# Second feed-forward projection of an encoder layer: its operands loaded three steps ahead, its rows by halves, and a longer fill before the first projection

## The chip, the core and the metric

One Trainium2 chip, one of its cores. The metric is the device time in microseconds (us) of one execution; lower is better. TensorE (PE) does matmuls, VectorE (DVE), ScalarE (ACT) and GpSimd (POOL) the elementwise work, SyncE (SP) issues every DMA.

## The reference, cut to what matters

One layer of a streaming encoder for 1024 prompt rows and 128 sample rows of 1024 columns, float32. The change lies in the last of its blocks:

```
x = LN(alpha*x + mixers(x) @ w_out)              # recurrence and sliding-window attention
x = LN(alpha*x + mem_attention(x))
g, u = split(x @ w_ffn_in)                       # 1024 -> 2 x 2816
y = LN(alpha*x + (silu(g) * u) @ w_ffn_out)      # 2816 -> 1024
```

## The kernel before, in words

Nine tiles of 128 rows: eight of the prompt (`TILES`), one of the samples (`SAMPLE`). Every float32 operand is split into a rounded part `hi` and a rest `lo` (`split`: ACT copies, DVE or POOL subtracts), and a product is three matmuls (`mm3`, L96). The feed-forward block works on the prompt by Strassen-Winograd products of halves: seven products stand for eight. So its operands are the blocks A11, A12, A21, A22 of the weights with sums S1 to S4, and B11, B21, B22 of the rows with differences T1 to T4.

The first projection runs over 11 pairs of column tiles (`PAIRS`), one `hidden(ops, i, then)` each: four loads of 512 KB (`a11`, `a21`, `a22`, `a12`), sums on POOL, then seven products of 24 matmuls of 512 columns. The sample rows go through plain matmuls of 128 columns without a split: for the pairs below `FILL` in `filler`, before `hidden(0)`, with weights loaded a second time through the three buffers `w_raw`; for the others in `sample_pair` inside `hidden`, with the weights that lie there. `all_operands` makes the row operands beforehand, four sets of transposes, copies and subtractions, interleaved with `filler` by planned times. The buffers `big` (10 of 4 KB a partition) hold the rows, the stages of the operands and the weights `a`. The activations are stored to `h_scratch` (B11 to T4) and `hs_scratch` (samples).

The second projection runs over parts of two or three pairs (`PARTS`). A part is a block for the rows (0, 1), the products of the samples, and a block for the rows (2, 3); in the last part the rows 2 and 3 have a block each. A block (`blocks`) goes through `steps`, seven products in the banks x, z and w; `operand` loads the product's operand from `h_scratch` into `hq` (2 buffers), ACT rounds it into `hh`, DVE or POOL subtracts into `hl`. After each product `add` adds the bank to the rows `y` on DVE (L1164); the next product that goes into the same bank waits for that. `prepare` loads the weights of a pair (`raw`, 2 x 512 KB), makes four sums on POOL (L1111 to L1114) and eight pairs of hi (ACT L1121) and lo (DVE or POOL L1122). The first two operands and the first two pairs are prepared inside `hidden(10)` by `ahead`.

Instructions stand on each engine, SP included, in a fixed order, which the program's builder chooses by times that it plans; they need not stand in the order of the source. An engine works through its order without overtaking.

## Time and profile before

| what | value |
|---|---|
| median of 3 runs | 1707.23 us (1706.56 to 1713.33) |
| the profiled execution's own time | 1704.64 us |
| its span, first to last instruction | 1702.9 us |
| PE, DVE, ACT, POOL busy | 1620.7, 1134.6, 674.4, 495.7 us |
| mean granted TensorE clock | 0.981 |

The trace is of one execution; outside its span lie 1.7 us. A clock of 1.00 is the level of 2.4 GHz, 0.50 that of 1.2 GHz.

### The profile page before, as it was taken

What the parts mean: (1) busy time and instruction counts of PE and PEld (TensorE: products, weight loads), DVE (VectorE), ACT (ScalarE), POOL (GpSimd) and SP (SyncE); (2) the same over time, 40 slices, a digit from 0 to 9 for tenths busy, and PEclk for the clock granted to TensorE, in tenths of its full rate; (3) what the DMA queues carried; (4) which work ended last, traced back from release to release, by engine and by line L of the source; (5) the groups of instructions that cost most, each with busy time, mean ns of one, the idle gap of its engine ahead of it and who ended that gap; (6) DMA issues with size and microseconds to landing.
All of it is one profiled execution on the core that took longest, in us unless ns stands there. A gap on an engine that the chain in (4) does not pass through costs nothing.

```text
span 1702.9 us, 24403 instructions
## 1 busy us (share of the span) xinstructions
PE 1620.7 (95%) x9065; PEld 1391.3 (82%) x9065; DVE 1134.6 (67%) x2021; ACT 674.4 (40%) x1365; POOL 495.7 (29%) x381
## 2 busy tenths in 40 slices
PE   8999999999999999999979999999999969988896
PEld 7998999999888987889877888888888857766674
DVE  6786788778488666786687454544444665767576
ACT  4543555446443544325263333323222333434321
POOL 1111111111000000000074443332333454676555
PEclk9999999999999999999998999999999988999998
DMA  7443343334974687556362333122222245333342
GB/s 239 143 160 122 102 148 104 98 118 137 314 274 154 197 278 268 198 171 236 115 205 78 104 115 117 66 74 86 95 92 96 93 164 180 105 118 118 103 146 95
DMA packets 114358, 247.91 MB, mean 146 GB/s; under 512 B 11840, under 2 KB 58048, under 8 KB 114240
## 3 DMA queue, kind: packets, MB, share of 16 engines
q1 hardware_dynamic: 114240, 246.36, 43.8%
q8 instruction: 71, 1.16, 0.3%
q14 instruction: 47, 0.39, 0.1%
HBM read 203.65 MB, written 42.60 MB: 145 GB/s over the span
## 4 chain that ended last, share of the span: by engine, by line
PE 77%; DVE 7%; DMA 6%; POOL 5%; ACT 2%; issue 2%; SPq 1%; POOLq 0%; ACTq 0%; DVEq 0%
PE a L96 48%; PE b L96 20%; PE x L96 3%; PE b L100 2%; DMA hq<-h_scratch 2%; PE z L96 1%; DVE w L1122 1%; PE s L96 1%; DMA raw<-in_w_f_dram 1%; PE w L96 1%; DVE y L1164 1%; DMA w_raw<-in_w_out_dram 1%; DMA w_raw<-in_w_fm_dram 1%; DMA w_raw<-in_w_f_dram 1%; DVE w_lo L137 1%
## 5 line engine op out<-in xcount | busy, mean ns | idle before, releaser
L137 DVE TENSOR_TENSOR w_lo<-w_raw,w_hi 128x1024 fp32r<-128x1024 f32 (+1 forms) x169 | 204.8, 1214 | 115.0 <-ACT w_hi L136 114.6
L136 ACT CAST w_hi<-w_raw 128x1024 fp32r<-128x1024 f32 (+1 forms) x169 | 174.6, 1034 | 206.1 <-PE a L96 77.4
L96 PE MATMUL a<-w_hi,q_hi 128*128 128x256 f32 (+1 forms) x576 | 197.4, 344 | 0.8 <-ACT kv_sb L270 0.7
L96 PE MATMUL a<-w_lo,q_hi 128*128 128x256 f32 (+1 forms) x576 | 196.9, 342 | 0.0
L96 PE MATMUL a<-w_hi,q_lo 128*128 128x256 f32 (+1 forms) x576 | 194.7, 338 | 0.0
L96 PE MATMUL a<-q_hi,w_hi 128*128 128x384 f32 x528 | 186.8, 354 | 7.3 <-ACT q_hi L136 4.3
L96 PE MATMUL a<-q_hi,w_lo 128*128 128x384 f32 x528 | 179.9, 341 | 0.0
L96 PE MATMUL a<-q_lo,w_hi 128*128 128x384 f32 x528 | 179.5, 340 | 0.0
L96 PE MATMUL x<-w,hh 128*128 128x512 f32 x344 | 115.0, 417 | 39.5 <-DVE y L1164 23.6
L137 DVE TENSOR_TENSOR w_lo<-a,w_hi 128x1024 fp32r<-128x1024 f32 x43 | 75.0, 1743 | 76.9 <-ACT w_hi L136 76.9
L96 PEld LDWEIGHTS a<-w_hi,q_hi 128*128 128x128 f32 x576 | 108.4, 188 | 15.6 <-ACT kv_sb L270 1.1
L96 PEld LDWEIGHTS a<-w_lo,q_hi 128*128 128x128 f32 x576 | 108.6, 189 | 13.3 <-issue 1.2
L96 PEld LDWEIGHTS a<-w_hi,q_lo 128*128 128x128 f32 x576 | 108.5, 188 | 12.7 <-issue 0.2
L96 PEld LDWEIGHTS x<-w,hh 128*128 128x128 f32 x344 | 66.6, 198 | 62.8 <-ACT hh L1152 15.7
L96 PEld LDWEIGHTS a<-q_hi,w_hi 128*128 128x128 f32 x528 | 100.5, 190 | 12.2 <-ACT q_hi L136 4.6
L699 POOL TENSOR_TENSOR rs<-rs,mhalf 128x1 f32<-128x1 f32 x18 | 17.2, 958 | 301.0 <-DVE rs L698 301.0
L96 PE MATMUL a<-T_h,w_hi 128*128 128x512 f32 x264 | 104.7, 396 | 0.0
L96 PE MATMUL a<-T_l,w_hi 128*128 128x512 f32 x264 | 104.7, 396 | 0.0
L96 PE MATMUL a<-T_h,w_lo 128*128 128x512 f32 x264 | 104.6, 396 | 0.0
L96 PEld LDWEIGHTS a<-q_lo,w_hi 128*128 128x128 f32 x528 | 100.7, 191 | 1.6 <-issue 0.9
L96 PEld LDWEIGHTS a<-q_hi,w_lo 128*128 128x128 f32 x528 | 100.2, 190 | 1.0 <-DVE w_lo L137 0.7
L1152 ACT CAST hh<-hq 128x512 fp32r<-128x512 f32 (+2 forms) x75 | 46.3, 619 | 133.2 <-DMA hq<-h_scratch 117.3
(308 smaller groups left out, 3930.4 us busy)
## 6 DMA issues: line engine op xcount, KB each, us to landing
a<-in_w_f_dram SPq DMA_DIRECT2D x44, 512.0 KB, 5.2
w_raw<-in_w_fm_dram SPq DMA_DIRECT2D x41, 512.0 KB, 3.9
h_scratch<-w_raw SPq DMA_DIRECT2D x55, 256.0 KB, 2.2
hq<-h_scratch SPq DMA_DIRECT2D x54, 256.0 KB, 2.7
w_raw<-in_w_tm_dram SPq DMA_DIRECT2D x24, 512.0 KB, 3.5
w_raw<-in_w_out_dram SPq DMA_DIRECT2D x24, 512.0 KB, 5.7
w_raw<-in_w_mq_dram SPq DMA_DIRECT2D x24, 512.0 KB, 4.2
w_raw<-in_w_mo_dram SPq DMA_DIRECT2D x24, 512.0 KB, 4.4
```

Of the source, the lines that this page charges most:

```text
L96: return self.eng.matmul(out, lhsT, rhs, **kw)
L100: return self.eng.transpose(out, in_, identity)
L136: S.copy(hi, src)
L137: V.tensor_tensor(lo, src, hi.bitcast(F32), op=ALU.subtract)
L699: G.tensor_tensor(rs, rs, mhalf[:, 0:1], op=ALU.pow)
L1122: (G if name in ("A21", "A22") else V).tensor_tensor(lo, src, hi.bitcast(F32), op=ALU.subtract)
L1152: S.copy(hi, q)
L1164: V.scalar_tensor_tensor(y[b, e][:, hs], y[b, e][:, hs], 1.0 if key in y else ALPHA, ps, op0=ALU.mult, op1=ALU.add)
```

## The change

`FILL` goes from 4 to 6: the samples of pairs 4 and 5 move from `hidden(4)` and `hidden(5)` into `filler`. `begin(0)`, the four weight loads of `hidden(0)` and the split of its first, is called before the last set of row operands. In `hidden(10)` the samples come after the last activation, and their store comes later, after the loads of the second projection's rows. These are loaded by halves in the order of use, with the first operand load after four of eight. `operand` becomes `load(n)`, `part_of(n)` and `operand()`: it loads up to three steps ahead of use and splits one step ahead, in a fixed list of turns, with five buffers `hq` of 2 KB a partition. In the last part, the rows 0 and 1 have a block each, as 2 and 3 had.

```diff
--- before.py
+++ after.py
@@ -31,7 +31,7 @@
 TILES = (0, 1, 3, 4, 5, 6, 7, 8)
 SAMPLE = 2
 PAIRS = FT // 2
-FILL = 4
+FILL = 6
 PARTS = ((0, 2), (2, 4), (4, 6), (6, 8), (8, 11))
 
 
@@ -950,16 +950,19 @@
             load(j)
         yield 3500.0
         for j in range(4):
+            if j == 3:
+                begun.append(begin(0))
             operands(ops, j, (got[j], got[j + 4]))
             yield 6000.0
         order.set(ready, 1000.0)
 
-    def sample_gated(i, h, g):
+    def sample_gated(i, h, g, store=True):
 
         S.activation(h, g[0], AF.Tanh, scale=0.5)
         V.scalar_tensor_tensor(h, h, 1.0, g[0], op0=ALU.add, op1=ALU.mult)
         V.scalar_tensor_tensor(h, h, 0.5, g[1], op0=ALU.mult, op1=ALU.mult)
-        nc.sync.dma_start(out=hs_dram[:, i], in_=h)
+        if store:
+            nc.sync.dma_start(out=hs_dram[:, i], in_=h)
 
     def filler(filled):
 
@@ -979,7 +982,7 @@
             yield
         order.set(filled)
 
-    def sample_pair(i, ws):
+    def sample_pair(i, ws, store=True):
 
         ps = bank("b")
         for e in range(2):
@@ -989,25 +992,34 @@
                              start=kt == 0, stop=kt == KT - 1)
         g = ps.rearrange("p (e z t) -> p z e t", e=2, z=2)
         h = hs.rearrange("p (e t) -> p e t", e=2)
-        sample_gated(i, h, [g[:, 0], g[:, 1]])
+        sample_gated(i, h, [g[:, 0], g[:, 1]], store)
 
     def parts_of(src, hi, lo):
         split(src, hi, lo)
         return hi, lo
 
+    begun = []
+
+    def begin(i):
+
+        def wt(name, j):
+            t = big(name)
+            nc.sync.dma_start(out=t, in_=I["w_f1"][i, j])
+            return t
+
+        a11, a21, a22, a12 = wt("a11", 0), wt("a21", 2), wt("a22", 3), wt("a12", 1)
+        return a11, a21, a22, a12, parts_of(a11, *both_parts())
+
+    def both_parts():
+        return tuple(wp.tile([P, 1024], F32R, name=x, bufs=N_W) for x in ("w_hi", "w_lo"))
+
     def hidden(ops, i, then):
 
-        def wt(name, j=None):
-            t = big(name)
-            if j is not None:
-                nc.sync.dma_start(out=t, in_=I["w_f1"][i, j])
-            return t
-
+        a11, a21, a22, a12, first = begun.pop() if begun else begin(i)
         th = [raw_tile() for _ in range(2)]
         m1 = raw_tile()
         m1 = [m1[:, :512], m1[:, 512:]]
-        a11, a21, a22, a12 = wt("a11", 0), wt("a21", 2), wt("a22", 3), wt("a12", 1)
-        s1, s2, s4 = wt("s1"), wt("s2"), wt("s4")
+        s1, s2, s4 = big("s1"), big("s2"), big("s4")
         G.tensor_tensor(s1, a21, a22, op=ALU.add)
         G.tensor_tensor(s2, s1, a11, op=ALU.subtract)
         G.tensor_tensor(s4, a12, s2, op=ALU.subtract)
@@ -1017,7 +1029,7 @@
         X, Z, W = [], [], []
 
         def product(bk, which, w, op, start):
-            pair = parts_of(w, *(wp.tile([P, 1024], F32R, name=x, bufs=N_W) for x in ("w_hi", "w_lo")))
+            pair = first if w is a11 else parts_of(w, *both_parts())
             for z in range(2):
                 if start:
                     bk.append(bank(which))
@@ -1043,7 +1055,7 @@
         last = i == PAIRS - 1
         if FILL <= i and not last:
             sample_pair(i, ((a11, a12), (a21, a22)))
-        s3 = wt("s3") if last else a21
+        s3 = big("s3") if last else a21
         G.tensor_tensor(s3, a11, a21, op=ALU.subtract)
         for z in product(Z, "b", s1, "T1", True):
             S.copy(m1[z], Z[z])
@@ -1071,12 +1083,12 @@
             store(o, src)
         for z in product(X, "a", a22, "T4", False):
             yield
-        if last:
-            sample_pair(i, ((a11, a12), (a21, a22)))
         gated(th[1][:, a], X[0], X[1])
         G.tensor_tensor(t4, th[1][:, a], t2, op=ALU.subtract)
         store("B21", th[1][:, a])
         store("T4", t4)
+        if last:
+            sample_pair(i, ((a11, a12), (a21, a22)), False)
 
     def final_norm(y, gb, st, b, e):
         mv, rs, nb = small("mv", 2), small("rs", 1), small("nb", 1)
@@ -1143,15 +1155,47 @@
         sums = [bank("s") for _ in range(2)]
         gb = []
 
-        def operand(i0, i1, bs, o):
-
-            k, n, c = i1 - i0, len(bs), bs[0] % 2
-            lo, q, hi = (f2.tile([P, 3, 2, P], t, name=x, bufs=m)[:, :k, :n]
-                         for x, t, m in (("hl", F32R, 5), ("hq", F32, 2), ("hh", F32R, 5)))
-            nc.sync.dma_start(out=q, in_=h_dram[bs[0] // 2, OPS.index(o), :, i0:i1, c:c + n])
-            S.copy(hi, q)
-            (G if o in ("T1", "T3", "T4") else V).tensor_tensor(lo, q, hi.bitcast(F32), op=ALU.subtract)
-            return [[(hi[:, i, b], lo[:, i, b]) for i in range(k)] for b in range(n)]
+        steps = (("x", "A11", "B11", True, (0, 0, None)),
+                 ("z", "S1", "T1", True, (1, 1, None)),
+                 ("x", "S2", "T2", False, (1, 0, None)),
+                 ("z", "S4", "B22", False, (1, 0, 1)),
+                 ("x", "S3", "T3", False, (1, 1, 1)),
+                 ("w", "A12", "B21", True, (0, 0, 0)),
+                 ("x", "A22", "T4", False, (0, 1, 0)))
+
+
+        turns = [(part, bs) for part in PARTS[:-1] for bs in ((0, 1), (2, 3))] + [(PARTS[-1], (b,)) for b in range(4)]
+        wanted = [(*part, bs, step[2]) for part, bs in turns for step in steps][2:]
+        loaded, parted = {}, {}
+
+        def load(n):
+            if n < len(wanted) and n not in loaded:
+                i0, i1, bs, o = wanted[n]
+                k, m, c = i1 - i0, len(bs), bs[0] % 2
+                q = f2.tile([P, 512], F32, name="hq", bufs=5)[:, :k * m * P].rearrange("p (i b x) -> p i b x", b=m, x=P)
+                nc.sync.dma_start(out=q, in_=h_dram[bs[0] // 2, OPS.index(o), :, i0:i1, c:c + m])
+                loaded[n] = q
+
+        def part_of(n):
+            if n < len(wanted) and n not in parted:
+                i0, i1, bs, o = wanted[n]
+                k, m, q = i1 - i0, len(bs), loaded[n]
+                hi, lo = (f2.tile([P, 512], F32R, name=x, bufs=5)[:, :k * m * P].rearrange("p (i b x) -> p i b x", b=m, x=P)
+                          for x in ("hh", "hl"))
+                S.copy(hi, q)
+                (G if o in ("T1", "T3", "T4") else V).tensor_tensor(lo, q, hi.bitcast(F32), op=ALU.subtract)
+                parted[n] = [[(hi[:, i, b], lo[:, i, b]) for i in range(k)] for b in range(m)]
+
+        used = [0]
+
+        def operand():
+            n = used[0]
+            used[0] += 1
+            for x in range(n, n + 4):
+                load(x)
+            for x in range(n, n + 2):
+                part_of(x)
+            return parted.pop(n)
 
         def add(b, e, half, ps, bn, which):
             hs = slice(half * 512, half * 512 + 512)
@@ -1167,21 +1211,13 @@
             if bn is not None:
                 V.bn_stats(bn[:, half], y[b, e][:, hs])
 
-        steps = (("x", "A11", "B11", True, (0, 0, None)),
-                 ("z", "S1", "T1", True, (1, 1, None)),
-                 ("x", "S2", "T2", False, (1, 0, None)),
-                 ("z", "S4", "B22", False, (1, 0, 1)),
-                 ("x", "S3", "T3", False, (1, 1, 1)),
-                 ("w", "A12", "B21", True, (0, 0, 0)),
-                 ("x", "A22", "T4", False, (0, 1, 0)))
-
         def blocks(part, bs, gb):
 
             ws = [prepared[i] for i in range(*part)]
             bk = {}
             bn = {(b, e): sm.tile([P, 2, 6], F32, name="bn", bufs=6) for b in bs for e in range(2)} if gb else {}
             for which, w, h, start, (e, half, fin) in steps:
-                for b, hs in zip(bs, ahead.pop((bs[0] + part[0], h), None) or operand(*part, bs, h)):
+                for b, hs in zip(bs, ahead.pop((bs[0] + part[0], h), None) or operand()):
                     if start:
                         bk[which, b] = bank(which)
                     ps = bk[which, b]
@@ -1222,16 +1258,22 @@
         for n, part in enumerate(PARTS):
             last = n == len(PARTS) - 1
             if n == 0:
-                for e in range(2):
+
+                for k, (e, half) in enumerate(((0, 0), (1, 1), (1, 0), (0, 1))):
+                    c2 = slice(half * 512, half * 512 + 512)
                     for b in range(2):
-                        nc.sync.dma_start(out=y[b, e], in_=x2_dram[TILES[b + 4 * e]])
+                        nc.sync.dma_start(out=y[b, e][:, c2], in_=x2_dram[TILES[b + 4 * e]][:, c2])
+                    if k == 1:
+                        load(0)
+                nc.sync.dma_start(out=hs_dram[:, PAIRS - 1], in_=hs.rearrange("p (e t) -> p e t", e=2))
             if last:
                 both = unit(c, "ln_gb").rearrange("p (n x) -> p n x", n=2)
                 gb = [both[:, n] for n in range(2)]
                 for n in range(2):
                     nc.sync.dma_start(out=gb[n], in_=I["ln"][4 + n:5 + n, :].broadcast_to([P, D]))
-            yield from blocks(part, (0, 1), gb)
-            hs = sample_operands(part)
+            for bs in ((0,), (1,)) if last else ((0, 1),):
+                yield from blocks(part, bs, gb)
+            hx = sample_operands(part)
             if n == 0:
                 for e in range(2):
                     for b in range(2, 4):
@@ -1239,7 +1281,7 @@
 
             while len(prepared) < min(part[1] + 1, PAIRS):
                 more()
-            yield from sample(part, hs, n == 0, last)
+            yield from sample(part, hx, n == 0, last)
             if last:
                 ys = unit(c, "ys")[:, :1024]
                 nc.sync.dma_start(out=ys, in_=x2_dram[SAMPLE])
```

## Rows read from the trace of the kernel before

**Rows 1.** The page: busy time of each engine in us, its share of the span, instructions.

```profile
PE 1620.7 (95%) x9065; PEld 1391.3 (82%) x9065; DVE 1134.6 (67%) x2021; ACT 674.4 (40%) x1365; POOL 495.7 (29%) x381
```

**Rows 2.** Busy time by stage: the stretch from the fill to the first steady product, the first projection, the change to the second, the second up to its last part's samples. Columns: stretch, its length, then busy us (instructions) of PE, PEld, DVE, ACT, POOL, granted clock, share and GB/s of the DMA engines.

```profile
884.60:902.80 18.20, 6.92 (x15) 5.01 (x16) 18.10 (x11) 6.79 (x10) 17.21 (x8) 0.62 0.60 184
902.80:1382.40 479.60, 479.60 (x2283) 395.49 (x2282) 248.94 (x256) 152.97 (x208) 183.10 (x96) 1.00 0.26 91
1382.40:1408.20 25.80, 10.56 (x37) 8.17 (x36) 11.41 (x16) 7.40 (x14) 11.13 (x9) 0.67 0.62 213
1408.20:1650.00 241.80, 217.80 (x883) 169.48 (x881) 163.40 (x220) 85.69 (x153) 146.64 (x99) 0.96 0.40 127
```

**Rows 3.** The chain that ended last, one of its pieces: start, us, what, number of matmuls.

```profile
1482.45 2.82 PE x L96 x12
```

**Rows 4.** Order of time around the start of the first projection: start, us, engine, line, operation, tiles, number, and in brackets the engine's idle time before it and what ended it.

```profile
883.58 1.35 SPq L1003 DMA_DIRECT2D a<-in_w_f_dram  x3
...
889.45 1.03 ACT L136 CAST w_hi<-a 128x1024 fp32r<-128x1024 f32 x1
...
890.53 0.80 PE L96 MATMUL a<-B_h,w_hi 128*128 128x512 f32 x1 [5.98 <-ACT w_hi L136]
...
894.96 2.52 DVE L137 TENSOR_TENSOR w_lo<-a,w_hi 128x1024 fp32r<-128x1024 f32 x1
...
897.53 0.80 PE L96 MATMUL a<-B_h,w_lo 128*128 128x512 f32 x1 [5.35 <-DVE w_lo L137]
```

**Rows 5.** The sample matmuls: two weight tiles of the fill, one pair inside `hidden`, PE's waits for the fill's loads (total, times, longest), and the fill's loads on the page (number, KB each, median us from issue to landing).

```profile
877.13 3.89 PE L96 MATMUL a<-both,w_raw 128*128 128x128 f32 x32 [0.58 <-DMA w_raw<-in_w_f_dram]
1375.12 7.31 PE L96 MATMUL b<-both,a 128*128 128x128 f32 x64
PE a L96 <- DMA w_raw<-in_w_f_dram: 1.7, 4, 0.6
w_raw<-in_w_f_dram SPq DMA_DIRECT2D x16, 512.0 KB, 4.2
```

**Rows 6.** Order of time at the change to the second projection: SP's issues, two of the row additions on DVE, the first new operand on ACT, PE.

```profile
1392.44 0.33 SPq L1227 DMA_DIRECT2D y<-x_scratch  x1
1393.82 0.33 SPq L962 DMA_DIRECT2D hs_scratch<-both  x1
1394.24 1.34 SPq L1227 DMA_DIRECT2D y<-x_scratch  x3
1395.63 1.28 SPq L1151 DMA_DIRECT2D hq<-h_scratch  x2
...
1399.28 0.69 DVE L1164 SCALAR_TENSOR_TENSOR y<-y,x 128x512 f32<-128x512 f32 x1 [2.71 <-DMA y<-x_scratch]
1400.58 0.69 DVE L1164 SCALAR_TENSOR_TENSOR y<-y,z 128x512 f32<-128x512 f32 x1 [0.61 <-DMA y<-x_scratch]
...
1402.47 1.30 ACT L1152 CAST hh<-hq 128x512 fp32r<-128x512 f32 x2 [9.60 <-DMA hq<-h_scratch]
...
1403.14 1.22 PE L96 MATMUL x<-w,hh 128*128 128x512 f32 x2 [15.24 <-ACT hh L1152]
```

**Rows 7.** SP's own waits at that place and in the second projection: total, times, longest.

```profile
SPq L1151 <- POOL hl L1153: 101.3, 30, 7.5
...
SPq L1036 <- POOL w_raw L1077: 6.3, 1, 6.3
...
SPq L1227 <- DMA h_scratch<-w_raw: 1.8, 1, 1.8
```

**Rows 8.** PE's waits in the second projection that follow a late operand, in order of time.

```profile
1432.21 0.70 PE L96 MATMUL x<-w,hh 128*128 128x512 f32 x2 [1.35 <-DVE y L1164]
1439.36 1.22 PE L96 MATMUL z<-w,hh 128*128 128x512 f32 x2 [2.70 <-DVE y L1164]
1453.00 0.71 PE L96 MATMUL x<-w,hh 128*128 128x512 f32 x2 [0.78 <-DVE y L1164]
1504.36 0.71 PE L96 MATMUL x<-w,hh 128*128 128x512 f32 x2 [2.23 <-DVE y L1164]
1557.24 0.71 PE L96 MATMUL x<-w,hh 128*128 128x512 f32 x2 [2.52 <-DVE y L1164]
1685.82 0.71 PE L96 MATMUL x<-w,hh 128*128 128x512 f32 x2 [1.84 <-DVE y L1164]
```

**Rows 9.** DVE just before the fifth of these waits ended, in order of time; then the half-clock stretches after the second and the fifth, as in Rows 2.

```profile
1554.13 0.69 DVE L1153 TENSOR_TENSOR hl<-hq,hh 128x512 fp32r<-128x512 f32 x1 [4.31 <-ACT hh L1152]
...
1556.42 0.67 DVE L1164 SCALAR_TENSOR_TENSOR y<-y,x 128x512 f32<-128x512 f32 x1
...
1438.70:1445.50 6.80, 6.14 (x15) 4.79 (x16) 4.30 (x8) 2.03 (x4) 4.96 (x4) 0.50 0.42 128
1559.00:1565.90 6.90, 6.20 (x16) 4.38 (x16) 4.46 (x6) 3.70 (x7) 6.38 (x6) 0.57 0.00 0
```

**Rows 10.** The lo parts of the weights (instructions; duration in ns, least, median, most; first and last start), PE's waits for the row additions after 1409 us (total, times, longest), and PE alone in two stretches of the last part: length, busy us (instructions), clock, share and GB/s of the DMA engines.

```profile
L1122 DVE TENSOR_TENSOR w<-s,w x44: 677/1114/1782, 1348.6 to 1615.9; 128x512 fp32r<-128x512 f32 x44
PE x L96 <- DVE y L1164: 23.6, 14, 5.6
1617.00:1650.00 33.00, 32.90 (x141) 1.00 0.49 153
1650.00:1692.00 42.00, 35.00 (x138) 0.96 0.29 99
```

## The prediction

> **What bounds the kernel now.** I read the page first. PE is busy for 95% of the span, DVE for 67%, no other engine for half [rows 1]. So time can be had only where PE stands still or runs at the lower clock, and I looked for these places with the table by stage [rows 2]. The first projection is full: 479.6 of 479.6 us at clock 1.00. What is taken out of it on PE is won, and nothing else there counts. Three stretches lose time. As a measure, 12 matmuls of 512 columns take 2.82 us at the full clock, 0.235 us each [rows 3].
>
> Ahead of the first projection, 15 matmuls ran in 18.2 us [rows 2]. They are worth 3.5 us; 14.7 us are lost. The order of time shows why: PE waits 5.98 us for the hi part of the first weights, whose loads are issued only at 883.58, then 5.35 us for their lo part, which DVE begins at 894.96, behind the last row operands [rows 4]. The rest is the lower clock, 0.62 on the mean.
>
> At the change to the second projection, 37 matmuls, worth 8.7 us, ran in 25.8 us at clock 0.67 [rows 2]; 17.1 us are lost. PE waits 15.24 us for the first operand that was not made beforehand. Its load stands on SP behind four loads of whole rows and the samples' store [rows 6], and these stand behind the store of the last activation difference [rows 7].
>
> In the second projection PE waits 23.6 us for row additions on x [rows 10]. DVE is not short of time there, 163.4 of 241.8 us [rows 2]; its order is the matter. Just before the fifth wait ended DVE had stood 4.31 us for a late `hh`, then did a subtraction, and the addition that PE wanted came at 1556.42 [rows 9]. Six waits follow such a late operand: 1.35 + 2.70 + 0.78 + 2.23 + 2.52 + 1.84 = 11.4 us [rows 8]. The operand is late because SP waits for one of two buffers: 101.3 us in 30 waits for POOL to release them [rows 7].
>
> **A, fill and first weights.** Two more pairs are eight weight tiles. Two tiles take 3.89 us on PE, so eight take 15.6 us; inside `hidden` a pair takes 7.31 us, so 14.6 us leave the full stage [rows 5]. Net cost 1.0 us. Against that, the 14.7 us go: PE now has work from 884.6 to about 900, while the last row operands and the split of the first weights end. That split, 1.03 us on ACT and 2.52 us on DVE [rows 4], now stands ahead of the last operands instead of behind; if it pushes them by its whole 2.52 us, they end at 894.96 + 2.52 = 897.5, still under the fill. With the cover gone it would cost those 3.6 us. What is late next is the loading. Four waits of 1.7 us stood in the fill of 16 tiles [rows 5]; with three buffers, a landing time of 4.2 us and 1.95 us of use a tile can come every 2.05 us, so eight tiles wait 0.8 us. The four weight loads of `begin` now share the queue with the fill: at 1.30 us for 512 KB (the spacing of two landings in [rows 6]) they take 5.2 us of it, of which I charge half, 2.6 us. A = 14.7 - 1.0 - 0.8 - 2.6 = 10.3, say 10 us. Upper bound 13.7 (loads hidden); lower bound 2, if all 5.2 us are felt and the `big` buffers that `begin` takes hold the last operands up by some 3 us more.
>
> **B, change to the second projection.** Ahead of the operand stand four halves, 1 MB in place of 2 MB: 2 x 1.30 = 2.6 us less. The samples' store no longer stands between the first and second load: SP ended the first issue at 1392.77 and made the second at 1394.24, 1.5 us later, against some 0.1 between others [rows 6]; 1.4 us less. B = 4.0 us; of the wait some 11 us stay, and the lower clock after it too, so I give nothing for that. Lower bound 0: the builder may put all halves first. Upper bound: if the first row half does not lie where the last difference lay, the loads no longer stand behind its store, for which SP waited 6.3 + 1.8 us [rows 7]; 4.0 + 8.1 = 12 us. The new moves cost ACT, DVE and PE nothing: the same products in the same banks.
>
> **C, loads three steps ahead.** Every operand then has its load issued three products early, 3 x 2.82 = 8.5 us, against a wait of at most 4.31 us [rows 9]. The six waits of 11.4 us can go, and the lower clock after two of them: 15 matmuls in 6.8 us lose 3.3 us, 16 in 6.9 us lose 3.1 us [rows 9], 0.7 of it a further wait; 5.7 us. Sum 17.1 us. But behind each operand on DVE stand lo parts of weights, of 1.1 us each [rows 10], which wait for POOL's sums and will be met earlier by the additions. I take two thirds, 11 us. Bounds 0 (they take the place of every wait) and 17. Of the 23.6 us on x, 8.7 belong to these six (the second is on z). The other 14.9 us, the longest wait of 5.6 among them [rows 10], follow weights or norms, not operands; I leave them.
>
> **D, single row blocks in the last part.** Rows 0 and 1 in pairs had PE busy for 32.90 of 33 us; the single blocks 2 and 3 for 35 of 42 [rows 10], 7 us short, with a step of cover fewer and the final norms on DVE and POOL beside. If the first two go the same way, it costs 7 us; with loads ahead and norms spread, perhaps nothing. I take 2 us.
>
> **Sum.** 10 + 4 + 11 - 2 = 23 us, from the profiled execution's 1704.64 to 1681.6, say 1682. That execution is 2.6 us under the median of the runs, 1707.23. A difference of 0.5% (8.5 us) is about what a measurement can tell from no change.
>
> **Rivals.** First: the weights take the place of the operands. DVE's lo parts take from 0.677 to 1.782 us for the same shape [rows 10], and an addition behind two of them is late however early the operand is. Then C is 0: 1704.64 - 12 = 1693 us. The same time results if SP, in its fixed order, stands behind weight loads whose buffers are not free, so that "three steps ahead" is not reached. For it: 14.9 of the 23.6 us are of other kinds already, most of this one. Against: the six waits begin with an idle DVE. The Trainium skill (SBUF — State Buffer, "Who interferes with whom") states that a DVE instruction with two SBUF inputs and a GpSimd instruction that reads SBUF block each other for a whole instruction. By that rule the moved subtractions meet POOL's sums as before and the result is this rival's; the spread of durations agrees with it, the idle DVE ahead of the waits doesn't depend on it.
>
> Second: the row halves are free of the last store, B = 12 and C near 17: 1704.64 - 10 - 12 - 17 + 2 = 1668 us. For it: only the first row load waited there for a store's landing, 1.8 us in one wait [rows 7]. Against: the order of SP's queue before.
>
> Third, the other side: the fill becomes a queue of loads. If each of the eight tiles came only 4.2 us after the tile before was used, they would take 8 x (4.2 + 1.95) = 49.2 us, with the four loads of `begin` 54.4, against 14.7 + 14.6 = 29.3 saved: 25.1 us lost, 12 after B, C and D, 1717 us. It decides from a tile time T where 8T + 5.2 - 29.3 exceeds the other 13 by 8.5 us: T = 5.7 us. Against: 1.7 us of waits in 16 tiles before.
>
> Fourth: nothing comes of it, A = 2 and the others near 0, about 1703 us.
>
> **How the numbers follow.** The forecast has 50%, with a range of its own of 1674 to 1689. The weights' rival has 22%, the free halves 20%, the fill 4%, nothing 4%. The range of 1665 to 1695 takes in the first rival and nearly all of the second and leaves out some 15%. Faster by over 0.5% are the forecast, the second rival and most of the first: 88%; within 0.5%, a small part of the first and the fourth: 8%; slower: 4%.
>
> **What would show it.** A: eight more weight tiles of the fill on PE and no wait of over 2 us before the first `B_h`; clock 1.00 there; the first projection shorter by 14 to 15 us. B: PE's wait at the change near 11 us, the operand's load fifth in its group on SP. C: waits of ACT for `hq` and of DVE for `hh` nearly gone, PE's waits for additions at 10 to 20 us. D: some more short waits of PE in the last part. The forecast is wrong if waits on additions stay above 25 us, if PE waits for `w_raw` by over 6 us, or if the wait at the change vanishes.

## The result, and the profile of the changed kernel

The changed kernel took 1697.77 us (median of 4 runs, 1695.56 to 1698.82), the kernel before 1709.0 beside it: ratio 0.9933, 95% interval 0.9918 to 0.9947. It is 0.7% faster, but the forecast was 1682 and the range ended at 1695. The profiled execution took 1695.56 us, its span is 1693.8, 9.1 less than before. One execution of a later kernel (e2_kept, 1976.13 us at a mean clock of 0.752) counts in no figure below.

The span is cut at five events that both traces show: PE's first matmul of the fill, its first of the second projection, its first on an operand that was loaded there, its last on the samples, its last of all.

| stretch | before | after | difference | predicted |
|---|---|---|---|---|
| start to first fill matmul (untouched) | 845.6 | 847.2 | +1.6 | 0 |
| fill to second projection (A) | 536.6 | 543.8 | +7.2 | -10 |
| second projection to first loaded operand (B) | 21.0 | 16.6 | -4.4 | -4 |
| to PE's end (C and D) | 289.3 | 275.6 | -13.7 | -9 |
| tail | 10.5 | 10.6 | +0.1 | 0 |

So B, C and D brought more than was forecast, and A, the largest gain but one, became a loss. The miss is A. Each kernel has one trace; where nothing was edited, the second stretch still differs by up to 2.8 us between kernels and the fourth by up to 5.3 (273.3 to 278.6), so smaller differences of a stretch prove nothing.

Busy time by stage of the changed kernel, columns as in [rows 2]: fill, end of the fill and first projection, change.

```profile
847.20:902.80 55.60, 48.51 (x384) 47.36 (x383) 45.59 (x40) 28.32 (x51) 39.19 (x25) 0.91 0.66 221
902.80:1391.00 488.20, 478.10 (x2236) 392.89 (x2234) 249.32 (x259) 153.42 (x209) 196.83 (x96) 0.99 0.28 97
1391.00:1412.40 21.40, 10.55 (x39) 8.16 (x38) 9.91 (x13) 6.23 (x12) 10.36 (x9) 0.76 0.69 224
```

The fill itself now has gaps and a clock of 0.91. PE's waits in it (total, times, longest):

```profile
PE a L96 <- DMA w_raw<-in_w_f_dram: 17.2, 6, 10.1
```

Before it was 1.7 us in four [rows 5]; the waits of 5.98 and 5.35 us for the first weights [rows 4] are gone. What the fill's loads wait for stands among SP's waits, 870 to 925 us:

```profile
SPq L965 <- DVE both L963: 29.6, 5, 10.9
```

L965 is the store of a pair's activation. It waits 29.6 us for DVE, and every load behind it on SP waits too. The sum alone says little: the kernel before has 20.3 us of such waits in the same window, in three. What matters is which load stands behind the store, and how much PE has left to do. The longest case in order of time (start, us, engine, line, operation, tiles, number), first on POOL:

```profile
892.67 2.81 POOL L1023 TENSOR_TENSOR s<-a,a 128x1024 f32<-128x1024 f32 x1
895.56 2.69 POOL L1024 TENSOR_TENSOR s<-s,a 128x1024 f32<-128x1024 f32 x1
```

DVE in the same time:

```profile
893.18 2.85 DVE L940 TENSOR_TENSOR B_l<-stage,B_h 128x512 fp32r<-128x512 f32 x1
895.95 2.84 DVE L940 TENSOR_TENSOR T_l<-tt,T_h 128x512 fp32r<-128x512 f32 x1
898.72 2.84 DVE L940 TENSOR_TENSOR B_l<-stage,B_h 128x512 fp32r<-128x512 f32 x1
901.48 5.57 DVE L137 TENSOR_TENSOR w_lo<-s,w_hi 128x1024 fp32r<-128x1024 f32 x2
906.97 0.41 DVE L962 SCALAR_TENSOR_TENSOR both<-both,a 128x256 f32<-128x256 f32 x1
907.30 1.21 DVE L137 TENSOR_TENSOR w_lo<-s,w_hi 128x1024 fp32r<-128x1024 f32 x1
908.44 0.41 DVE L963 SCALAR_TENSOR_TENSOR both<-both,a 128x256 f32<-128x256 f32 x1
```

SP, with the store and the loads of the fill around it, and above it the store before that one:

```profile
884.14 0.33 SPq L965 DMA_DIRECT2D hs_scratch<-both  x1
884.51 0.93 SPq L1007 DMA_DIRECT2D a<-in_w_f_dram  x2
885.54 12.34 SPq L974 DMA_DIRECT2D w_raw<-in_w_f_dram  x5
...
897.55 0.33 SPq L974 DMA_DIRECT2D w_raw<-in_w_f_dram  x1
908.87 0.33 SPq L965 DMA_DIRECT2D hs_scratch<-both  x1
909.30 1.34 SPq L974 DMA_DIRECT2D w_raw<-in_w_f_dram  x3
```

And PE, from its pace before to the three long waits of the fill, with other lines left out:

```profile
873.81 3.74 PE L96 MATMUL a<-both,w_raw 128*128 128x128 f32 x32
879.68 3.65 PE L96 MATMUL a<-both,w_raw 128*128 128x128 f32 x16 [2.13 <-DMA w_raw<-in_w_f_dram]
890.94 12.16 PE L96 MATMUL a<-both,w_raw 128*128 128x128 f32 x80 [4.07 <-DMA w_raw<-in_w_f_dram]
913.43 9.35 PE L96 MATMUL a<-both,w_raw 128*128 128x128 f32 x64 [10.10 <-DMA w_raw<-in_w_f_dram]
```

Read from the end: PE waits 10.10 us for a load issued at 909.30, right behind the store at 908.87, which waits for the activation's last step on DVE (L963). ACT had done its part (L961) at 899.23, but DVE was at the last row subtractions, 2.84 us each while POOL sums the early weights, and then at three lo parts of these sums, two ahead of L962 and one ahead of L963. From 897.55 to 908.87 SP issues nothing. The wait of 4.07 us ends with a load issued at 885.54; ahead of it on SP stand the store at 884.14 and two early weight loads.

The waits cost more than their length. The 160 matmuls right behind them took 25.2 us, at granted clocks of 0.53, 0.76 and 0.80; at the pace of the 32 in 3.74 us at 873.81 (clock 1.00) they would take 18.7.

### The profile page after: what moved, and what is told of

Same layout as the page of the kernel before. It is cut to its first block, busy times and chain, and to the rows that moved or that the text cites. A ratio compares the mean times of both kernels' runs of the same rounds, so it can differ in the third digit from the quotient of the medians.

```text
span 1693.8 us, 24482 instructions
## 1 busy us (share of the span) xinstructions
PE 1623.0 (96%) x9065; PEld 1397.5 (83%) x9065; DVE 1129.9 (67%) x2025; ACT 676.9 (40%) x1372; POOL 503.8 (30%) x384
## 4 chain that ended last, share of the span: by engine, by line
PE 77%; DVE 9%; POOL 5%; DMA 4%; issue 3%; ACT 2%; SPq 1%; POOLq 0%; ACTq 0%; DVEq 0%
PE a L96 48%; PE b L96 20%; PE x L96 3%; PE b L100 2%; PE z L96 2%; DMA raw<-in_w_f_dram 1%; DVE w L1134 1%; PE s L96 1%; DVE w_lo L137 1%; DVE T_l L940 1%; POOL s L1123 1%; DVE B_l L940 1%; PE w L96 1%; POOL s L1124 1%; DVE y L1208 1%
## 5 line engine op out<-in xcount | busy, mean ns | idle before, releaser
L96 PE MATMUL x<-w,hh 128*128 128x512 f32 x344 | 114.3, 415 | 26.6 <-DVE y L1208 15.5
L1185 ACT CAST hh<-hq 128x512 fp32r<-128x512 f32 (+1 forms) x82 | 47.1, 582 | 83.7 <-PE x L96 42.4
```

The lines of the kernel that those rows point to most:

```text
L96: return self.eng.matmul(out, lhsT, rhs, **kw)
L1185: S.copy(hi, q)
```

## The experiments

Each kernel is compared with the kernel before on the same chip; medians there were 1704.2 to 1706.5 us. "Stretch" is the second row of the table, from the first fill matmul to the second projection.

### A's two halves apart

Fill of six pairs alone, on the kernel before (e3_fill6_alone):

```diff
-FILL = 4
+FILL = 6
```

> The kernel before with FILL at 6 and nothing else. Store theory: without the early weights no lo parts stand ahead of the samples' steps on DVE during the fill; the fill waits less than 5 us for its loads, PE still waits some us for the first weights behind it, and the time is 1699 to 1704 us. Queue theory: the eight added tiles wait as in the changed kernel, 10 us or more, and the time is 1709 us or above.

Early first weights with the old fill, on the changed kernel (e1_fill4):

```diff
-FILL = 6
+FILL = 4
```

> The changed kernel with FILL back at 4; all else as changed. Theory (store theory): in the changed kernel the fill's last weight loads stand on SP behind the stores of the samples' activations, and these wait for DVE, whose last steps for the samples stand behind lo parts of the first weights; so the two added pairs cost 10 us of waiting and win 14.6 us less 15 us of the same work, a net loss. Then with FILL 4 the wait of 10.1 us is gone, the two shorter ones (2.1 and 4.1 us) stay, from the first fill matmul to the second projection 534 to 538 us in place of 543.8, and the time is about 1690 us against 1697.8. Rival (the early weights do the harm, not the longer fill): no faster than the changed kernel, 1696 to 1700 us.

The changed kernel with the first weights late again (e6_late_begin):

```diff
-            if j == 3:
-                begun.append(begin(0))
```

> The changed kernel with begin(0) called inside hidden(0) again, so the four weight loads and the first split are not early; fill stays at six pairs. Theory: the early weights let POOL make the first sums (L1023, L1024, L1059) while DVE does the last row subtractions, which then take 2.84 us each in place of 0.68 to 1.76, and put the sums' lo parts on DVE ahead of the samples' activations whose store blocks the fill's weight loads on SP. Without that the stretch from the first fill matmul to the second projection is that of the run with fill 6 alone, 528.7 us in place of 543.8: 1697.8 - 15 = 1683 us (1679 to 1687). Rival: the length of the fill and the split of the loads ahead, not the early weights, hold the changed kernel back; then no difference, 1695 to 1699 us.

Measured: e3 1698.7 us (ratio 0.9952, 0.9933 to 0.9971), e1 1688.91 (0.9888, 0.9866 to 0.991), e6 1682.02 (0.9866, 0.9851 to 0.988). e1 and e6 came near what was expected. e3 came out a little below its range, and one thing was read wrongly: with six pairs alone, no wait for the first weights is left, all 5.6 us are for `w_raw`. The stretch, with the sum of PE's waits between 840 and 960 us:

| kernel | fill | first weights | stretch | PE's waits |
|---|---|---|---|---|
| before | 4 | late | 536.6 | 13.1 |
| e3_fill6_alone | 6 | late | 528.7 | 5.6 |
| e1_fill4 | 4 | early | 533.6 | 9.9 |
| after | 6 | early | 543.8 | 17.2 |
| e6_late_begin | 6 | late | 528.6 | 8.0 |
| e7_first_early | 6 | a11 early | 528.6 | 6.4 |
| e12_three_early | 6 | a21 late, the rest early | 538.3 | 13.4 |
| e2_kept | 6 | early, activations kept | 534.8 | 11.5 |

Either half alone gains, 7.9 us the fill and 3.0 the early weights (hardly more than unchanged stretches differ); together they lose 7.2. They are two covers for one hole, and the second one stands in the way of the first. Without it the kernel takes 1682 us. Of the 15.2 us between the changed kernel and e6, PE's waits make 9.2; the rest is the lower clock behind them, since the fill of e6 ran at 1.00 and the matmuls behind its three longest waits lost 0.5 us in place of 6.5. DVE of e6_late_begin at the place shown above:

```profile
894.37 0.68 DVE L940 TENSOR_TENSOR B_l<-stage,B_h 128x512 fp32r<-128x512 f32 x1
894.98 0.41 DVE L960 SCALAR_TENSOR_TENSOR both<-both,a 128x256 f32<-128x256 f32 x1
895.49 0.42 DVE L961 SCALAR_TENSOR_TENSOR both<-both,a 128x256 f32<-128x256 f32 x1
895.83 1.22 DVE L137 TENSOR_TENSOR w_lo<-a,w_hi 128x1024 fp32r<-128x1024 f32 x1
```

SP of e6_late_begin, and its waits for the stores, 870 to 925 us:

```profile
876.21 6.37 SPq L972 DMA_DIRECT2D w_raw<-in_w_f_dram  x4
885.43 0.33 SPq L963 DMA_DIRECT2D hs_scratch<-both  x1
...
895.93 0.33 SPq L963 DMA_DIRECT2D hs_scratch<-both  x1
896.35 0.88 SPq L972 DMA_DIRECT2D w_raw<-in_w_f_dram  x2
SPq L963 <- DVE both L961: 21.5, 5, 6.7
```

The row subtraction takes 0.68 us, the activation follows at once, and the loads leave SP at 896.35 instead of 909.30. The split of the first weights lies under the fill here as well, without being asked to.

### Which part of the early weights does the harm

The changed kernel, the fill's activations kept in two buffers, one each of the four for hi and for lo parts of the weights, and stored after hidden(0) (e2_kept):

```diff
+        kept.extend(wp.tile([P, 1024], F32, name=x, bufs=N_W)[:, :768].rearrange("p (i e t) -> p i e t", e=2, t=P)
+                    for x in ("w_hi", "w_lo"))
...
-            h = hs.rearrange("p (e t) -> p e t", e=2)
-            sample_gated(i, h, [x.rearrange("p (e t) -> p e t", e=2) for x in ps])
+            sample_gated(i, kept[i // 3][:, i % 3], [x.rearrange("p (e t) -> p e t", e=2) for x in ps], False)
...
+            if i == 0:
+                for j in range(2):
+                    nc.sync.dma_start(out=hs_dram[:, 3 * j:3 * j + 3], in_=kept[j])
```

> The changed kernel with the samples' activations of the six fill pairs kept in two spare buffers of the weights' parts and stored after the first pair of the first projection; no store stands on SP inside the fill. Store theory: PE's waits for the fill's loads fall from 17.2 us to 5 or less, and the time to about 1686 us. Rival (queue theory: eight more tiles of 512 KB and the four early weight loads are too much for the DMA queue and the three buffers): the waits stay above 10 us and the time at 1695 to 1699 us.

Only a11 early (e7_first_early):

```diff
-        a11, a21, a22, a12 = wt("a11", 0), wt("a21", 2), wt("a22", 3), wt("a12", 1)
-        return a11, a21, a22, a12, parts_of(a11, *both_parts())
+        a11 = wt("a11", 0)
+        return wt, a11, parts_of(a11, *both_parts())
...
+        a21, a22, a12 = wt("a21", 2), wt("a22", 3), wt("a12", 1)
```

> The changed kernel with only the first of the four weight tiles (a11) loaded and split early; the other three are loaded in hidden(0). POOL then has nothing to sum while DVE ends the row operands. If POOL's sums and their lo parts are the harm, it comes out with the kernel that begins late, 1679 to 1687 us, and perhaps 1 to 2 us better since the first lo part is off the path. If an early lo part ahead of the last operands is already harmful (the weight loads' place in the queue, or the first split), it comes out between, 1688 to 1698 us.

All early but a21, without which POOL can make no sum (e12_three_early; the lines that hand a21 over are left out):

```diff
-        a11, a21, a22, a12 = wt("a11", 0), wt("a21", 2), wt("a22", 3), wt("a12", 1)
+        a11, a22, a12 = wt("a11", 0), wt("a22", 3), wt("a12", 1)
...
+        a21 = wt("a21", 2)
```

> The changed kernel with three of the four early weight loads as they are (a11 with its split, a22, a12) and only a21 loaded in hidden(0). Every sum of the weights needs a21, so POOL makes none of them while DVE ends the row operands, but three quarters of the early loads stand in the queue. Theory (the early sums, their weight on DVE's subtractions and their lo parts ahead of the samples' activations do the harm): like the kernel that begins late, 1680 to 1687 us, row subtractions on DVE back at 0.7 to 1.8 us and no wait of PE for the fill's weights over 5 us. Rival (the early loads take the queue from the fill's loads, as the term for loads in the prediction had it): most of the 15 us stay lost, 1690 to 1698 us, with long waits of PE for w_raw.

Measured: e2 1688.79 us (ratio 0.9895, 0.9867 to 0.9923), e7 1684.37 (0.9882, 0.9858 to 0.9906), e12 1692.25 (0.9932, 0.9915 to 0.9948). Taking the stores out of SP's way gives 9.0 of the 15.2 us back (543.8 to 534.8), so the store in the queue is most of it. PE's waits for the fill's loads are 5.2 us there, the longest 2.8; the other 6.3 us are for parts of the first weights, whose buffers the edit cuts from four to three, so they may be of its own making.

One early load and its split do no harm (e7). e12 did not behave as I expected: the row subtractions are back at 0.68 to 1.76 us, yet only 5.5 us of the stretch return, and the time lies in the range of the rival. ACT of e12_three_early shows one reason:

```profile
908.06 1.04 ACT L136 CAST w_hi<-s 128x1024 fp32r<-128x1024 f32 x1 [5.53 <-POOL s L1026]
909.01 0.38 ACT L961 ACTIVATE both<-a 128x256 f32<-128x256 f32 x1
```

SP of e12_three_early behind it:

```profile
911.25 0.33 SPq L965 DMA_DIRECT2D hs_scratch<-both  x1
911.68 0.37 SPq L974 DMA_DIRECT2D w_raw<-in_w_f_dram  x1
```

The sums start as soon as a21 has landed, which is still inside the fill, and their hi parts now stand on ACT ahead of the activation, which waits 5.53 us for POOL behind one of them; then store, load and a wait of PE of 3.78 us follow as before.

The other long wait of e12 (4.73 us, ended at 891.78) has another reason, and so has the wait of 4.07 us in the changed kernel. Between the second and the third store of the fill, four loads leave on SP in each of these kernels: four of the fill in e6 (the line at 876.21), three and a11 in e7, two and two early weight loads in the changed kernel and in e12. The fill's loads that are displaced leave behind the third store: the one that PE waits for in e12 at 887.26, behind a store at 886.36 for which SP had waited 7.6 us. That store itself was not late: it followed the fill's first matmul by 37.9 us, in e6 by 37.0. A crowded DMA queue explains little of this: the fill's loads landed after a median of 4.4 us in both kernels and 4.2 in e6.

So the harm isn't the slow subtractions as such. Early weights harm in two ways, both through a store of the samples on SP: their loads push loads of the fill behind it (4.07 and 4.73 us), and the parts of their sums delay it on DVE or ACT (10.10 and 3.78 us). That a store is in the way is shown by e2; the split between the two ways is read from the traces, and no run has the second without the first.

### C and D

The changed kernel, operands loaded and split at their use again (e5_at_use):

```diff
-                q = f2.tile([P, 512], F32, name="hq", bufs=5)[:, :k * m * P].rearrange("p (i b x) -> p i b x", b=m, x=P)
+                q = f2.tile([P, 512], F32, name="hq", bufs=2)[:, :k * m * P].rearrange("p (i b x) -> p i b x", b=m, x=P)
...
-            for x in range(n, n + 4):
+            for x in range(n, n + 1):
...
-            for x in range(n, n + 2):
+            for x in range(n, n + 1):
```

> The changed kernel with part C undone: each operand of the second projection is loaded and split in the product that uses it, with two buffers hq; everything else as changed. Theory from the trace after and from the single-blocks run: stage from the first loaded operand to PE's end lost 13.7 us although the single blocks cost 2 to 4 us, so the loads ahead are worth 16 to 17 us, and this kernel takes about 1697.8 + 16 = 1714 us (1709 to 1718), with waits of DVE for hh back at some 40 us. Rival, the first of the prediction in weak form: the loads ahead are worth the predicted 11 us or less and the rest is due to the later stores and row halves; then 1705 to 1709 us.

The kernel before, rows 0 and 1 in single blocks in the last part (e4_single_alone):

```diff
-            yield from blocks(part, (0, 1), gb)
+            for bs in ((0,), (1,)) if last else ((0, 1),):
+                yield from blocks(part, bs, gb)
```

> The kernel before with one block each for the rows 0 and 1 in the last part and nothing else. The prediction's term D: 2 us slower (0 to 7), about 1711 us. Rival (the norms of rows 0 and 1 begin earlier and lie apart, so DVE and POOL are freer in the last blocks): the stretch from the last sample product to PE's end, 38.0 us before and 32.0 in the changed kernel, falls by 4 to 6 us, about 1704 us.

And e6_late_begin with these rows in one block (e10_paired):

```diff
-        turns = [(part, bs) for part in PARTS[:-1] for bs in ((0, 1), (2, 3))] + [(PARTS[-1], (b,)) for b in range(4)]
+        turns = [(part, bs) for part in PARTS[:-1] for bs in ((0, 1), (2, 3))] + [(PARTS[-1], bs) for bs in ((0, 1), (2,), (3,))]
...
-                q = f2.tile([P, 512], F32, name="hq", bufs=5)[:, :k * m * P].rearrange("p (i b x) -> p i b x", b=m, x=P)
+                q = f2.tile([P, 768], F32, name="hq", bufs=4)[:, :k * m * P].rearrange("p (i b x) -> p i b x", b=m, x=P)
...
-            for bs in ((0,), (1,)) if last else ((0, 1),):
-                yield from blocks(part, bs, gb)
+            yield from blocks(part, (0, 1), gb)
```

> The kernel that begins late, with part D undone: rows 0 and 1 in one block in the last part, which needs buffers of 3 KB (768 columns), four of each kind instead of five. Theory: D costs what the run of it alone showed, 3.6 us (2 to 5), so this takes 1682.0 - 3.6 = 1678.4 us (1677 to 1680). Rival: with operands loaded ahead the single blocks cost nothing, or four buffers bring waits back: 1681 to 1686 us.

Measured: e5 1715.75 us (ratio 1.0061, 1.0042 to 1.0079), e4 1710.48 (1.0021, 1.0009 to 1.0034), e10 1688.17 (0.9888, 0.9871 to 0.9904). The waits on late operands in the second projection of the changed kernel (total, times, longest):

```profile
ACT hh L1185 <- DMA hq<-h_scratch: 10.8, 3, 5.3
DVE hl L1186 <- ACT hh L1185: 9.8, 7, 1.9
```

The same of e5_at_use:

```profile
ACT hh L1185 <- DMA hq<-h_scratch: 118.1, 36, 7.6
DVE hl L1186 <- ACT hh L1185: 47.6, 20, 4.5
```

The loads ahead take the lateness away, and without them it is back; in the kernel before these waits were 117.3 and 42.4 us. The stretch from the first loaded operand to PE's end is 275.6 us with them, 296.1 without (e5) and 289.3 before. So C is worth 13.7 us from the one side and 20.5 from the other; why e5 is 6.8 us longer there than the kernel before isn't settled.

For D the medians mislead. In the same stretch e4 takes 289.0 us against 289.3, and e10 275.7 against the 275.7 of e6: single blocks cost nothing that shows, with or without loads ahead, and pairing the rows again didn't bring the 3.6 us that I expected from e4's median. e4's time is the expected one by luck: what e4 and e10 have more lies mostly ahead of the fill, where nothing was edited: 849.2 and 852.6 us against 845.6 and 848.4 (the last section). Inside the stretch two things cancel. From the last sample product to PE's end, single blocks are shorter: 35.7 us for 37.6 in e4, where the rival expected 4 to 6 less, and 31.6 (e6) for 33.9 (e10). Ahead of it they are longer by 1.6 and 2.4 us.

### What is left of B

e6_late_begin with the last difference T4 on DVE instead of POOL in hidden(10) (e8_t4_dve):

```diff
-        G.tensor_tensor(t4, th[1][:, a], t2, op=ALU.subtract)
+        (V if last else G).tensor_tensor(t4, th[1][:, a], t2, op=ALU.subtract)
```

> The kernel that begins late, and in hidden(10) alone the difference T4 is made by DVE instead of POOL, where it stood behind four sums of the second pair's weights (1391.64 to 1397.21). If SP's fixed order behind the store of T4 is what holds the first operand's load, the store is issued some 5 us earlier and PE's wait of 10.9 us at the change falls to about 6 us: 4 to 6 us less than the kernel that begins late, 1677 to 1679 us. If the row halves or the landing of the loads themselves bound the wait, it changes by less than 1.5 us.

e6_late_begin with a third operand made inside hidden(10) (e9_third_ahead):

```diff
-            for n, o in enumerate(OPS[:2]):
+            for n, o in enumerate(OPS[:3]):
...
-        wanted = [(*part, bs, step[2]) for part, bs in turns for step in steps][2:]
+        wanted = [(*part, bs, step[2]) for part, bs in turns for step in steps][3:]
```

> The kernel that begins late, with the third operand of the second projection (T2 of the first pairs, stored long before) loaded and split inside hidden(10) as the first two are; the loads that follow are one step further on. Theory: of the 10.6 us that PE waits at the change, the operand's load on SP behind the store of T4 and four row halves is the cause, so the wait for hh goes; but the first row half, issued at the same place, lands only 11.9 us after the first product (1402.8 against 1391.0 in the changed kernel), and the addition to it must come before the third product goes into bank x, so a wait of 6 to 8 us stays: 3 to 5 us less than the kernel that begins late, 1677 to 1679 us. Rival: the additions don't wait for the rows as much as I read, or the whole wait goes: 1671 to 1674 us. Other rival: the extra loads and splits in hidden(10) delay the first pairs' weights, no gain.

e9_third_ahead and e10_paired together (e11_both); the edits are the two diffs above:

> Both edits together, third operand made ahead and rows 0 and 1 paired in the last part, on the kernel that begins late. They lie in different stretches, so their gains should add: 1682 - 4 - 3.6 = 1674.4 us (1671 to 1678). If one of them gains nothing alone, this comes out with the other.

Measured: e8 1682.91 us (ratio 0.9864, 0.985 to 0.9879), e9 1681.14 (0.9859, 0.9831 to 0.9886), e11 1680.61 (0.9844, 0.9827 to 0.986), all within 1.5 us of e6, where 3 to 8 were expected. At the change PE waited 10.6 us in e6 and 8.3 in e8, whose last store left 2.1 us earlier after the first product and not the expected 5. In e9 the wait for the operand is gone, and PE waits for a row addition instead. SP of e9_third_ahead:

```profile
1384.15 0.36 SPq L1046 DMA_DIRECT2D h_scratch<-w_raw  x1
1384.61 1.85 SPq L1264 DMA_DIRECT2D y<-x_scratch  x4
```

PE of e9_third_ahead, the third product:

```profile
1388.82 0.76 PE L96 MATMUL x<-w,h 128*128 128x512 f32 x1 [5.20 <-DVE y L1207]
```

The addition needs the first row half, which stands on SP behind the store of T4 like the operand did and landed at 1387.91; DVE was at other work until 1387.95 as well. From the second projection's start to PE's end e8 and e9 took 289.8 and 290.1 us against 292.1, and the stretch ahead of it came out 2.7 and 2.2 us longer, no more than it differs between kernels that are alike there. Nothing here is faster than e6 by more than can be measured; e11 has the lowest median, 26 us under the kernel before.

## Why the prediction was wrong, by its steps

**A, wrong: the failed step is the price of "what is late next is the loading", 0.8 and 2.6 us.** The loads were priced by landing time, use and their share of the queue, as if a load left as soon as its buffer was free. On SP a store of the samples stands ahead of them, and it waits for DVE. The landing time was right (a median of 4.4 us for 4.2); the order of issue was left out. The early weight loads pushed loads of the fill behind a store, and the parts of the early sums delayed a store. The prediction named the split of the first weights as work ahead of the last operands, 2.52 us, and asked only what it does to these operands. It didn't ask who waits for DVE through SP, and it counted only that split: with all four tiles early, the sums on POOL and their parts on ACT and DVE come early too. The lower clock behind such waits, 6 of the 15.2 us, had no term. Its lower bound of 2 us allowed for 3 us of held buffers, not for a stall of 10, and its own terms give 14.7 - 1.0 - 0.8 - 5.2 - 3 = 4.7. The sign named in advance, PE waiting for `w_raw` by over 6 us, is what came: 17.2. The hole of 14.7 us was real: six pairs of fill alone closed 7.9 of it and left no wait for the first weights, so the early weights had nothing left to cover.

The trace of before already held the sign. There the first weights' loads, issued at 883.58 [rows 4], leave right behind such a store, for which SP had waited 6.2 us:

```profile
883.16 0.33 SPq L962 DMA_DIRECT2D hs_scratch<-both  x1
```

The third rival foresaw the place and not the mechanism. Its queue needed 6.15 us for each tile; here 16.3 of the 17.2 us are three waits (2.13, 4.07 and 10.10) for loads issued within 1.4 us of such a store. Not all of that is due to the change: e6 has waits of 1.34, 1.31 and 3.43 us near these places.

The row subtractions went from at most 1.76 us to 2.84 while POOL's sums ran beside them, each starting 0.4 to 0.5 us after a sum's start and ending 0.55 us after its end. The Trainium skill (SBUF — State Buffer, "Who interferes with whom") states that such a pair blocks for a whole instruction; the trace agrees. It was weighed in the prediction for the second projection, and it bit in the fill. By e12, which has the short subtractions and most of the loss, it is the smaller part.

**B, right in size, its two terms only in part.** 4.4 us for 4.0; PE waited 10.85 us where "near 11" was said, and the operand's load stood fifth. In the changed kernel POOL makes four sums for the next weights before T4 (1391.64 to 1397.21), and SP holds everything behind its store.

SP of the changed kernel, the three stores, four row halves and the operand:

```profile
1391.70 7.60 SPq L1048 DMA_DIRECT2D h_scratch<-w_raw  x3
1399.41 1.85 SPq L1265 DMA_DIRECT2D y<-x_scratch  x4
1401.30 0.43 SPq L1176 DMA_DIRECT2D hq<-h_scratch  x1
```

ACT and PE:

```profile
1406.90 0.62 ACT L1185 CAST hh<-hq 128x512 fp32r<-128x512 f32 x1 [5.34 <-DMA hq<-h_scratch]
1407.57 0.79 PE L96 MATMUL x<-w,hh 128*128 128x512 f32 x1 [10.85 <-ACT hh L1185]
```

From the first row load's issue to the operand's it is 1.89 us in place of 3.19 [rows 6], 1.3 for the 1.4 of the store; from there to the rounding on ACT 5.6 in place of 6.84, 1.2 for the 2.6 of the halved bytes. Most of the rest comes from the second rival: the halves no longer wait 1.8 us for the store's landing [rows 7]. Its larger part falls: they are still issued behind the store, for which SP waits as before.

**C, near in size, wrong in mechanism at half of the places.** Apart from the wait at the change, PE's waits in the second projection fell from 30.7 to 20.3 us by the view of waits, 10.4 us where six had been priced at 11.4. The other 3.3 of the 13.7 us are clock and gaps too short to count as waits, where 5.7 had been priced. Two thirds of 17.1 was a cut for lo parts that would take the operands' place. PE's waits for additions in the changed kernel, 1408 us to the end:

```profile
PE x L96 <- DVE y L1208: 15.5, 7, 3.1
PE z L96 <- DVE y L1208: 4.2, 4, 1.4
```

On x they fell from 23.6 [rows 10] to 15.5, nearly by the 8.7 that belonged to late operands. But these did not simply go. Of the six waits of [rows 8] the first and the last are gone and the second is 1.35 us for 2.70. At the other three, PE waits for the next addition instead, in the next product:

| place | before: late operand, next product | after: the same |
|---|---|---|
| third | 0.78, 1.42 | 0, 2.52 |
| fourth | 2.23, 1.41 | 0, 2.63 |
| fifth | 2.52, 0.70 | 0, 2.81 |

There 1.1 of 5.5 us were won. The next product at the third place, before:

```profile
1456.29 0.73 PE L96 MATMUL x<-w,hh 128*128 128x512 f32 x2 [1.42 <-DVE y L1164]
```

POOL, ACT, DVE and PE there in the changed kernel:

```profile
1452.20 1.29 POOL L1123 TENSOR_TENSOR s<-raw 128x512 f32<-128x512 f32 x1 [2.67 <-DMA raw<-in_w_f_dram]
1453.52 0.62 ACT L1133 CAST w<-s 128x512 fp32r<-128x512 f32 x1 [3.15 <-POOL s L1123]
1454.17 1.08 DVE L1134 TENSOR_TENSOR w<-s,w 128x512 fp32r<-128x512 f32 x1 [2.50 <-ACT w L1133]
1455.18 0.68 DVE L1208 SCALAR_TENSOR_TENSOR y<-y,x 128x512 f32<-128x512 f32 x1
1455.91 0.73 PE L96 MATMUL x<-w,hh 128*128 128x512 f32 x2 [2.52 <-DVE y L1208]
```

The addition stands on DVE behind a lo part of the weights, which waits through ACT and POOL for a weight load. That is the first rival, the weights in the operands' place, and it held at three of six places; e6 has 1.87, 2.31 and 2.56 us there. The six places with what followed them gave 5.6 of the 10.4 us. The rest came from waits that the prediction had left alone: the longest fell from 5.57 to 3.08 us, and short ones near the end went; why isn't shown. That C's sum came near is in part luck.

**D, mis-sized at +2:** 0, as far as unchanged stretches of this length agree (273.3 to 278.6 us). The cost that it named may be there ahead of the samples (1.6 and 2.4 us, no more than unchanged code varies); what it left out is that the blocks behind them become shorter by as much (1.9 and 2.4 us).

**Sum.** -10, -4, -11 and +2 were said; +7.2, -4.4, -13.7 and 0 came, and +1.6 from the part ahead. A alone is off by 17 us. With A as in e6 the kernel takes 1682.02 us, the number forecast for the whole change, but not by its terms: there A is -7.9, B -4.6, C and D -13.6, and the part ahead +2.8.

## What to carry to other kernels

Ask of each load not only when its buffer is free, but which store stands ahead of it on the issuing queue and on which engine that store waits; then ask what the change puts in front of that engine's last step, and which loads it pushes behind that store. Two edits that fill the same hole are priced together, not one by one: here each gained alone and both lost. A wait that goes at one product can come back at the next, behind whatever stands next in the engine's order: count it as won only once that has been looked up.

## What the runs showed that was not expected

The part ahead of the fill, the same instructions in all fourteen kernels, took 845.6 to 852.6 us. In the slowest, most of the difference arises near 160 to 180 us, where the same work ran at a different granted clock. The kernel before, columns as in [rows 2]:

```profile
160.00:180.00 20.00, 20.00 (x144) 16.92 (x145) 10.29 (x25) 4.62 (x16) 3.72 (x5) 0.91 0.20 67
```

e10_paired:

```profile
160.00:180.00 20.00, 20.00 (x114) 16.23 (x114) 7.09 (x16) 3.72 (x12) 1.14 (x2) 0.66 0.12 37
```

PE did 144 matmuls in these 20 us at a clock of 0.91 and 114 at 0.66; at the first pace the 30 that are missing take 4.2 of the 6.9 us between the two kernels. The clock there doesn't explain all of the spread: e8 and e12 have 0.91 as well and are 3 us longer than the kernel before. All four runs of e10 lay 5.4 to 7.2 us over e6's median (1687.42 to 1689.23), and its other stretches differ by 2.0 us in all, so it seems to belong to the kernel and not to one execution; why isn't known (e9 and e11, on the same chip, don't show it). A median that moves by 3 or 4 us is therefore no proof of an edit's worth, and the stretch that the edit touches has to be read by itself.
